# Layer 1's modulation vectors: from TensorE products in its branches to VectorE row sums in the two feed-forward loops

## The chip, the cores and the metric

One core of a Trainium2 chip runs the kernel. The metric is the device time of one execution in microseconds, as a median over runs. The engines are named as the profile names them: PE (TensorE matmul, with PEld for its weight loads), DVE (VectorE), ACT (ScalarE), POOL (GpSimd) and SP (SyncE, which here issues nearly all DMAs).

## The reference

Two layers of a diffusion backbone work on 384 tokens (256 latent, 128 context) of width 1024, in float32. Six modulation vectors of 1024 values, each in two versions (context `c_ctx` and latent `c`), steer a layer:

```python
mod_ctx = (jax.nn.silu(c_ctx) @ w_mod[l] + b_mod[l])[None, :]
mod_lat = jax.nn.silu(c) @ w_mod[l] + b_mod[l]
sh1, sc1, g1, sh2, sc2, g2 = [m[:, None, :] for m in jnp.split(mod, 6, axis=-1)]
h = layer_norm(x) * (1 + sc1) + sh1
x = layer_norm(ALPHA * x + g1 * (merged @ p["w_o"]), p["ln1_g"], p["ln1_b"])
h = layer_norm(x) * (1 + sc2) + sh2
x = layer_norm(ALPHA * x + g2 * ((jax.nn.silu(ug) * uv) @ p["w_down"]), p["ln2_g"], p["ln2_b"])
```

`merged` is the gated sum of three branches (attention, convolution module, Fourier mixing). `ug` and `uv` are the halves of a width-3 convolution of `h @ w_up` (2 x 2816 wide). The modulation depends on `c` and the weights alone, so it can be computed at any time before its use.

## The kernel before, in words

Every large product is made of three fp32r products of high and low halves (`mm3`, L196 to L198). The halves of a weight tile come from `halves`: ACT writes the high half (L179), DVE the low one (L180). Weight tiles come in through SP into 3 buffers `raw` of 1 MB; 5 buffers each hold high and low halves.

A layer has a mixing part (`mixing`) and a feed-forward part (the rest of `layer`). The mixing part makes the input projection, then three branches of eight steps each (`branch`); scores, values and the convolution (62 instructions of DVE a layer, L783 and L785) are written in between the steps. Then come the product with `w_o`, a closing normalization (`close`, L817 to L828) of three token tiles, and the feed-forward loop of 11 units. A unit makes four tiles of `w_up` (24 products each, `ws_tile`, into 2 PSUM buffers `ps`), empties each by ACT (L927) and DVE (L928, L930), gates them (L945 to L951) and multiplies with two row blocks of `w_down` (`down`). The products of the last five row blocks are held back (`TAIL`), to run between the end of the loop and `close`.

The modulation is computed in three ways. Kind A is shift and scale of the mixing part, B those of the feed-forward part, G the two gates.

- Layer 0, kind A: at the start, on PE (`mod_first`).
- Kinds G and B of both layers: in the branches of the same layer, on PE (`mod_stream`, L217). A step is 8 multiplications with a 32-column left side, which the profile shows as 16 matmuls; every second step of a branch calls one. Its weights come as 256 KB tiles into buffers `s2`. Gates go through a DRAM tile (`mod_gates`, L268 to L276, into `gscr`), from where `gate_bc` reads them back, spread over 128 partitions, before each `close`; shift and scale are copied (L282), transposed on PE (L286) and get their bias (L294).
- Layer 1, kind A: row sums on DVE in layer 0's feed-forward loop (`mod_rows`, L315). The weights lie transposed; one instruction multiplies a 128 x 1024 tile with `silu(c)`, spread over the partitions, and sums each row. There are 16 tiles with two sums each, so 32 sums. `next(rows, None)` takes one tile in each half unit from unit 2 on. The weights come as 512 KB tiles into two buffers, a fetch two tiles ahead.

`silu(c)` is made in `setup`: a load of `c2` (L145), DVE L146, ACT L147, DVE L148. It is written to DRAM (`cscr`, L154) for the row sums. That write stands in SP's queue between the loads of the tokens and those of all weights.

Each engine takes its instructions in a fixed order. The order is set before the run by a planner (the Tile framework), which goes by the order of writing but lets a later instruction pass where it takes an engine to be free and the later one to be ready. Buffers are handed out by tag (`s4` has 8, `ps` 2, `acc` 6); an instruction that needs a buffer waits until its last user is done.

Of the kernel before, what the change touches and what calls it, by code (L numbers as in the profile page):

```python
# [16 lines left out]
P = 128  # L17
# [60 lines left out]
class Net:  # L78
# [3 lines left out]
    def __init__(self, ctx, tc, a):  # L82
# [5 lines left out]
        self.modcol, self.bmod, self.colsets = {}, {}, {}  # L88

# [41 lines left out]
    def setup(self):  # L131
# [22 lines left out]
        nc.sync.dma_start(self.cscr.rearrange("v (k p) -> (v k) p", p=P), ch)  # L154
# [141 lines left out]
    def mod_rows(self, l, kind):  # L296

        nc, a = self.nc, self.a
# [3 lines left out]
        b0 = 3 if kind == "B" else 0  # L302
        tiles = [(j, k) for j in range(2) for k in range(KD)]
        sums = [self.sm(16) for _ in range(2)]

        def fetch(n):
            j, k = tiles[n]
            self.load(w[n % 2], a["w_modr"][l - 1, self.MODS[kind], j, k])
# [4 lines left out]
        for n, (j, k) in enumerate(tiles):  # L313
            for v in range(2):
                nc.vector.scalar_tensor_tensor(prod, w[n % 2], 1.0, cb[v], op0=ALU.mult, op1=ALU.mult,  # L315
                                               accum_out=sums[j][:, v * KD + k:v * KD + k + 1])
            if n + 2 < len(tiles):
                fetch(n + 2)
            if k == KD - 1:
                for v in range(2):  # L320
                    nc.vector.tensor_tensor(self.modcol[l][:, j + (2 if kind == "B" else 0), v, :],
                                            sums[j][:, v * KD:(v + 1) * KD], self.bmod[l][:, j + b0, :], op=ALU.add)
            yield

# [184 lines left out]
    def mixing(self, l, first, hT, mods):  # L509
# [63 lines left out]
        mods = self.mod_stream(mods)  # L573
# [3 lines left out]

        ci = conv_in()
# [23 lines left out]
        for i, _ in enumerate(branch(1, 0, "w_a", 4, aT, lambda: values(3))):  # L602
            next(cb, None)
            if i % 2:
                mod()
        for i, _ in enumerate(branch(2, 1, "w_c", 2, cT, lambda: [None for _ in cb])):
            if i % 2:
                mod()
        for _ in mods:
            pass  # L610
        return m_hl
# [233 lines left out]
    def layer(self, l, first, hT, mods):  # L845
        nc, a = self.nc, self.a
        m_hl = self.mixing(l, first, hT, mods)
# [59 lines left out]
        rows = self.mod_rows(l + 1, "A") if l + 1 < DEPTH else iter(())  # L907
# [188 lines left out]
```

## Time and profile before

| | |
|---|---|
| median of 3 runs | 1163.52 us (1162.24 to 1163.95) |
| the profiled execution | 1162.13 us, span 1160.3 us |
| PE busy | 1139.3 us (98%) |
| DVE busy | 785.1 us (68%) |
| ACT busy | 522.9 us (45%) |
| POOL busy | 77.5 us (7%) |

The span runs from the first to the last instruction; the time has some 1.8 us around it. Times in rows are microseconds from the span's start. PE is busy nearly all the time, so a microsecond of PE work that is taken out is one that can be won, if no other engine then stands in the way in the same stretch. In the stretch tables, a column is an engine's busy time with its number of instructions, then the clock granted to PE (1.00 is full), the mean busy share of the 16 DMA engines and their rate. In a timeline, a row is start, duration, engine, line, operation, and in brackets the idle time before it with what ended it.

### The profile page before, as it was taken

The page shows a single profiled execution, that of the slowest core. Times are in us where ns is not written, and L with a number is a line of the kernel's source. Part 1 is how long each engine was busy: PE and PEld are TensorE (multiplying, and loading weights), DVE is VectorE, ACT ScalarE, POOL GpSimd, SP SyncE. Part 2 cuts the span into 40 slices and gives each one's busy share as a digit, 9 for nine tenths or more (in the row PEclk, how much of TensorE's full clock was granted, in tenths as well). Part 3 has the DMA queues.
Part 4 walks back from the last instruction along what each step waited for, and adds up shares of the span by engine and source line. Part 5 has one row for each costly group of instructions (what it writes and reads, how often), then busy time and mean ns, then how long its engine had stood idle before and what let it go on. Part 6 is the DMA issues. An engine that isn't in the chain of part 4 may idle for free.

```text
span 1160.3 us, 16670 instructions
## 1 busy us (share of the span) xinstructions
PE 1139.3 (98%) x6569; PEld 1019.4 (88%) x6569; DVE 785.1 (68%) x1332; ACT 522.9 (45%) x875; POOL 77.5 (7%) x91
## 2 busy tenths in 40 slices
PE   8999999999999999999999999999999999999996
PEld 6788888898999999999958978889989999999995
DVE  5579965445799976666776799444477666555667
ACT  2457743242754344444372766233447444334440
POOL 1010001121100000000021000111110000000001
PEclk9999999999999999999999999999999999999998
DMA  9764567633366663343335364783427333333411
GB/s 362 295 205 145 167 229 271 231 141 127 128 236 206 229 206 139 109 136 119 110 122 216 118 218 155 277 313 109 146 73 251 112 114 141 113 142 109 146 37 55
DMA packets 47806, 195.95 MB, mean 169 GB/s; under 512 B 5552, under 2 KB 6608, under 8 KB 32624
## 3 DMA queue, kind: packets, MB, share of 16 engines
q1 hardware_dynamic: 47296, 194.10, 47.3%
q8 instruction: 52, 0.85, 0.3%
q10 hardware_dynamic: 432, 0.79, 0.2%
q14 instruction: 26, 0.21, 0.0%
HBM read 191.41 MB, written 3.45 MB: 168 GB/s over the span
## 4 chain that ended last, share of the span: by engine, by line
PE 84%; DVE 8%; ACT 2%; DMA 2%; POOL 1%; issue 1%; SPq 0%; POOLq 0%; DVEq 0%; ACTq 0%
PE ps L196 16%; PE ps L198 16%; PE ps L197 16%; PE acc L196 9%; PE acc L197 9%; PE acc L198 9%; PE acc L217 2%; PE acc L767 1%; DVE sm L372 1%; DVE wlo L180 1%; POOL sm L376 1%; DVE s L818 1%; DVE s L828 1%; PE acc L755 1%; ACT whi L179 1%
## 5 line engine op out<-in xcount | busy, mean ns | idle before, releaser
L180 DVE TENSOR_TENSOR wlo<-raw,whi 128x1024 fp32r<-128x1024 f32 x216 | 269.1, 1247 | 236.2 <-ACT whi L179 227.2
L196 PE MATMUL ps<-hT,whi 128*128 128x386 f32 (+1 forms) x1088 | 370.3, 340 | 1.8 <-ACT g L548 1.5
L198 PE MATMUL ps<-hT,wlo 128*128 128x386 f32 (+1 forms) x1088 | 368.7, 339 | 0.0
L197 PE MATMUL ps<-hT,whi 128*128 128x386 f32 (+1 forms) x1088 | 368.4, 339 | 0.0
L179 ACT CAST whi<-raw 128x1024 fp32r<-128x1024 f32 x216 | 225.8, 1049 | 308.1 <-PE ps L197 211.4
L196 PEld LDWEIGHTS ps<-hT,whi 128*128 128x128 f32 x1088 | 205.2, 189 | 14.1 <-ACT whi L179 5.0
L197 PEld LDWEIGHTS ps<-hT,whi 128*128 128x128 f32 x1088 | 205.2, 189 | 2.7 <-issue 1.7
L198 PEld LDWEIGHTS ps<-hT,wlo 128*128 128x128 f32 x1088 | 205.3, 189 | 0.3 <-issue 0.3
L197 PE MATMUL acc<-wlo,r 128*128 128x512 f32 x360 | 142.3, 395 | 0.0
L196 PE MATMUL acc<-whi,r 128*128 128x512 f32 x360 | 142.1, 395 | 0.0
L198 PE MATMUL acc<-whi,r 128*128 128x512 f32 x360 | 141.9, 394 | 0.0
L198 PEld LDWEIGHTS acc<-whi,r 128*128 128x128 f32 x360 | 67.6, 188 | 16.2 <-DVE r L951 0.5
L196 PEld LDWEIGHTS acc<-whi,r 128*128 128x128 f32 x360 | 67.6, 188 | 14.9
L197 PEld LDWEIGHTS acc<-wlo,r 128*128 128x128 f32 x360 | 67.6, 188 | 14.4
L785 DVE SCALAR_TENSOR_TENSOR cv<-upad,cst,cv 128x399 f32<-128x399 f32 x120 | 70.1, 627 | 0.1
L376 POOL TENSOR_TENSOR sm<-sm,mhalf 128x1 f32<-128x1 f32 x21 | 23.0, 1099 | 612.4 <-DVE sm L375 611.7
L950 ACT CAST r<-g 128x386 fp32r<-128x386 f32 x44 | 22.7, 515 | 89.5 <-DVE g L948 89.5
L927 ACT ACTIVATE g<-ps,cst 128x386 f32<-128x386 f32 x84 | 56.3, 670 | 0.0
L930 DVE SCALAR_TENSOR_TENSOR g<-ps,cst,g 128x385 f32<-128x385 f32 x84 | 52.0, 619 | 2.3
L928 DVE SCALAR_TENSOR_TENSOR g<-ps,cst,g 128x385 f32<-128x385 f32 x84 | 51.6, 614 | 0.2
L563 POOL TENSOR_TENSOR g<-g,g 128x384 f32<-128x384 f32 x32 | 35.8, 1118 | 181.8 <-DVE g L562 173.3
L945 ACT ACTIVATE g<-g 128x386 f32<-128x386 f32 x44 | 23.2, 527 | 45.2 <-DVE g L930 45.2
(185 smaller groups left out, 1353.0 us busy)
## 6 DMA issues: line engine op xcount, KB each, us to landing
raw<-w_u SPq DMA_DIRECT2D x44, 1024.0 KB, 4.8
s<-w_mod SPq DMA_DIRECT2D x128, 256.0 KB, 4.4
raw<-w_g SPq DMA_DIRECT2D x24, 1024.0 KB, 7.8
raw<-w_d SPq DMA_DIRECT2D x22, 1024.0 KB, 4.9
raw<-w_mod SPq DMA_DIRECT2D x8, 1024.0 KB, 9.5
raw<-w_o SPq DMA_DIRECT2D x8, 1024.0 KB, 4.8
s<-w_modr SPq DMA_DIRECT2D x16, 512.0 KB, 4.2
s<-w_z SPq DMA_DIRECT2D x8, 512.0 KB, 9.7
```

Of the source, the lines that this page charges most:

```text
L179: self.nc.scalar.copy(hi, raw)
L180: self.nc.vector.tensor_tensor(lo, raw, f32(hi), op=ALU.subtract)
L196: mm(ps, lh, rh, start=first, stop=False)
L197: mm(ps, lh, rl, start=False, stop=False)
L198: mm(ps, ll, rh, start=False, stop=last)
L217: self.nc.tensor.matmul(ps[32 * i:32 * i + 32, 0:n], self.cpad[:, k, :], src[k, i], start=ks[0] == 0 and k == ks[-1], stop=ks[-1] == KD - ...
L376: nc.gpsimd.tensor_tensor(mv[:, 3:4], mv[:, 2:3], self.mhalf, op=ALU.pow)
L563: nc.gpsimd.tensor_tensor(merged[m], merged[m], gt, op=ALU.add)
L785: nc.vector.scalar_tensor_tensor(c, u[:, i:i + CV_W], w, c, op0=ALU.mult, op1=ALU.add)
L927: nc.scalar.activation(c, ps, AF.Identity, bias=cols["ffn_b"][:, i:i + 1], scale=w[1])
L928: nc.vector.scalar_tensor_tensor(c[:, 1:NPAD], ps[:, 0:NPAD - 1], w[0], c[:, 1:NPAD], op0=ALU.mult, op1=ALU.add)
L930: nc.vector.scalar_tensor_tensor(c[:, 0:NPAD - 1], ps[:, 1:NPAD], w[2], c[:, 0:NPAD - 1], op0=ALU.mult, op1=ALU.add)
```

## The change

- `mods` for layer 1 is now empty: no `mod_stream` in its branches.
- `mod_rows` takes a list of units (layer, kind, which of the pair), each of 8 tiles and 16 sums. In layer 0's loop there are five: A 0, A 1, G 0, B 0, B 1, so 80 sums. In layer 1's loop there is one: G 1, so 16 sums. `mix_rows` (sums in the branches) is empty.
- `paced` spreads the steps over slots, one slot for each half unit from unit 1 on: 41 steps (the first only fetches) over 17 slots in layer 0, 9 steps over 9 slots in layer 1.
- `gate_rows` turns the sums of a gate into rows: a transpose on PE, a copy on ACT, an 8 KB write to `gscr`. It is called in the last unit of either feed-forward loop.
- The write of `cscr` moves from `setup` to `setup_late`, which comes after the loads of the input projection.

```diff
-        nc.sync.dma_start(self.cscr.rearrange("v (k p) -> (v k) p", p=P), ch)
+        self.silu = ch
...
     def setup_late(self):
         nc, a = self.nc, self.a
+        nc.sync.dma_start(self.cscr.rearrange("v (k p) -> (v k) p", p=P), self.silu)
...
+    def gate_rows(self, tag):
+
+        nc = self.nc
+        for l, j, cols in self.gate_sums:
+            pt = self.psum(tag)[0:2 * KD, 0:P]
+            nc.tensor.transpose(pt, cols, self.ident)
+            row = self.kk()[0:2 * KD, :]
+            nc.scalar.copy(row, pt)
+            nc.sync.dma_start(self.gscr[l, j].rearrange("v (k p) -> (v k) p", p=P), row)
+        self.gate_sums = []
+
+    def paced(self, units, slots):
+
+        steps = self.mod_rows(units) if units else iter(())
+        need, done = len(units) * KD + 1, [0, 0]
+
+        def step():
+            done[0] += 1
+            while done[1] * slots < need * done[0]:
+                done[1] += 1
+                next(steps, None)
+
+        return step
...
-        rows = self.mod_rows(l + 1, "A") if l + 1 < DEPTH else iter(())
+        step_rows = self.paced(rows, 17 if len(rows) > 1 else 9)
...
-                if u >= 2:
-                    next(rows, None)
+                if u >= 1:
+                    step_rows()
             if u >= 1:
                 down(u - 1)
+            if u == KF // 2 - 1:
+                self.gate_rows("ps")
         down(KF // 2 - 1)
         gate = self.gate_bc(l, 1)
...
-        mods = [[(0, "G"), (0, "B")], [(1, "G"), (1, "B")]]
+        mods = [[(0, "G"), (0, "B")], []]
+        mix_rows = [[], []]
+        ffn_rows = [[(1, "A", 0), (1, "A", 1), (1, "G", 0), (1, "B", 0), (1, "B", 1)], [(1, "G", 1)]]
```

## Rows read from the trace of the kernel before

**Rows 1.** The page's first part.

```profile
PE 1139.3 (98%) x6569; PEld 1019.4 (88%) x6569; DVE 785.1 (68%) x1332; ACT 522.9 (45%) x875; POOL 77.5 (7%) x91
```

**Rows 2.** Layer 1's branches by stretch: PE, PEld, DVE, ACT, POOL, clock, DMA share, GB/s.

```profile
664.00:720.00 56.00, 55.27 (x356) 46.35 (x355) 53.22 (x122) 37.87 (x95) 0.00 (x0) 1.00 0.56 188
720.00:792.00 72.00, 71.58 (x444) 61.58 (x443) 35.70 (x55) 25.76 (x39) 10.17 (x12) 1.00 0.71 256
```

**Rows 3.** The same stretches, L217 alone (PE busy, PEld busy).

```profile
664.00:720.00 56.00, 6.18 (x48) 1.05 (x48) 1.00 0.56 188
720.00:792.00 72.00, 9.62 (x80) 2.09 (x80) 1.00 0.71 256
```

**Rows 4.** Timeline of PE, the end of layer 1's modulation.

```profile
788.73 0.66 PE L286 MATMUL acc<-ident,s 128*128 128x128 f32 x4 [0.39 <-DVE s L282]
```

**Rows 5.** Busy times by stretch in layer 0's feed-forward loop, columns as in rows 2.

```profile
338.00:419.30 81.30, 81.30 (x425) 75.85 (x424) 77.98 (x126) 33.33 (x45) 0.00 (x0) 1.00 0.64 218
...
444.64:469.96 25.32, 25.32 (x133) 23.71 (x133) 15.23 (x20) 10.46 (x15) 0.00 (x0) 1.00 0.36 124
```

**Rows 6.** L315 alone in the first of these stretches (DVE busy, two records a sum).

```profile
338.00:419.30 81.30, 34.26 (x56) 1.00 0.64 218
```

**Rows 7.** Groups by line and shape, DVE, 325 to 570 us: the two records of a row sum.

```profile
L315 DVE SCALAR_TENSOR_TENSOR s<-s,s 128x1024 f32<-128x1024 f32 x29 | 35.2, 1216 | 0.1
...
L315 DVE DVE_READ_ACCUMULATOR s<-s,s 128x1 f32 x29 | 2.4, 81 | 0.0
```

**Rows 8.** Timeline of DVE: one row sum and its successor.

```profile
338.06 1.22 DVE L315 SCALAR_TENSOR_TENSOR s<-s,s 128x1024 f32<-128x1024 f32 x1
339.20 0.08 DVE L315 DVE_READ_ACCUMULATOR s<-s,s 128x1 f32 x1
339.20 0.56 DVE L948 TENSOR_TENSOR g<-g,g 128x386 f32<-128x386 f32 x1
```

**Rows 9.** Timelines, start of layer 0's feed-forward loop: first sum (DVE), first loop product (PE).

```profile
318.91 1.23 DVE L315 SCALAR_TENSOR_TENSOR s<-s,s 128x1024 f32<-128x1024 f32 x1 [0.65 <-DMA s<-w_modr]
...
324.97 0.42 PE L196 MATMUL ps<-hT,whi 128*128 128x386 f32 x1 [0.33 <-DVE g L930]
```

**Rows 10.** Timeline of SP's queue at the start.

```profile
2.12 0.43 SPq L121 DMA_DIRECT2D s<-x_p  x1
5.53 0.33 SPq L154 DMA_DIRECT2D cscr<-kk  x1
5.90 0.42 SPq L121 DMA_DIRECT2D s<-par  x1
```

**Rows 11.** Timeline of PE at the start, and busy times of this stretch (columns as in rows 2).

```profile
13.82 1.08 PE L217 MATMUL ps<-raw,cpad 128*32 128x128 f32 x32 [1.20 <-DMA raw<-w_mod]
...
19.06 0.51 PE L196 MATMUL acc<-whi,hT 128*128 128x512 f32 x1 [0.86 <-ACT hT L416]
...
10.86:19.06 8.20, 4.23 (x76) 2.81 (x77) 5.79 (x22) 3.37 (x6) 0.55 (x1) 1.00 1.01 422
```

**Rows 12.** Timelines at the end of layer 1's loop (PE, ACT, DVE).

```profile
1129.30 0.34 PE L198 MATMUL ps<-hT,wlo 128*128 128x386 f32 x1
...
1130.45 0.67 ACT L927 ACTIVATE g<-ps,cst 128x386 f32<-128x386 f32 x1
...
1135.32 0.69 DVE L817 TENSOR_TENSOR s<-acc,s 128x512 f32<-128x512 f32 x1 [0.58 <-PE acc L198]
...
1150.66 0.69 DVE L817 TENSOR_TENSOR s<-acc,s 128x512 f32<-128x512 f32 x1 [0.26 <-PE acc L198]
```

**Rows 13.** Busy times by stretch between these two L817, columns as in rows 2.

```profile
1135.30:1150.60 15.30, 15.30 (x66) 12.04 (x65) 14.76 (x24) 0.00 (x0) 3.04 (x2) 1.00 0.14 50
```

**Rows 14.** DMA issues: count, size of one, median us from issue to landing; one tile's extremes.

```profile
s<-gscr SPq DMA_DIRECT2D x8, 512.0 KB, 6.5
...
o_xs<-s SPq DMA_DIRECT2D x2, 256.0 KB, 2.1
...
DMA to landing us min/median/max: 4.1/6.5/7.3
```

More of the change, by code (lines that the diff above doesn't have):

```diff
@@ L301, in mod_rows, with fetch @@
         w = [self.s4() for _ in range(2)]
[L302 to L308, printed above, removed]
+        tiles = [(n, k) for n in range(len(units)) for k in range(KD)]
+        sums = [self.sm(16) for _ in units]
+        def fetch(i):
+            n, k = tiles[i]
+            l, kind, j = units[n]
+            self.load(w[i % 2], self.a["w_modr"][l, self.MODS[kind], j, k])
         fetch(0)
@@ L312, in mod_rows @@
         yield
-        for n, (j, k) in enumerate(tiles):
+        for i, (n, k) in enumerate(tiles):
             for v in range(2):
[L315 to L318, printed above, removed]
+                nc.vector.scalar_tensor_tensor(prod, w[i % 2], 1.0, cb[v], op0=ALU.mult, op1=ALU.mult,
+                                               accum_out=sums[n][:, v * KD + k:v * KD + k + 1])
+            if i + 2 < len(tiles):
+                fetch(i + 2)
             if k == KD - 1:
+                l, kind, j = units[n]
+                bias = self.bmod[l][:, {"A": (0, 1), "B": (3, 4), "G": (2, 5)}[kind][j], :]
+                dst = sums[n] if kind == "G" else self.modcol[l][:, j + (2 if kind == "B" else 0)]
                 for v in range(2):
-                    nc.vector.tensor_tensor(self.modcol[l][:, j + (2 if kind == "B" else 0), v, :],
-                                            sums[j][:, v * KD:(v + 1) * KD], self.bmod[l][:, j + b0, :], op=ALU.add)
+                    d = dst[:, v * KD:(v + 1) * KD] if kind == "G" else dst[:, v, :]
+                    nc.vector.tensor_tensor(d, sums[n][:, v * KD:(v + 1) * KD], bias, op=ALU.add)
+                if kind == "G":
+                    self.gate_sums.append((l, j, sums[n]))
             yield
+    def gate_rows(self, tag):
+        nc = self.nc
+        for l, j, cols in self.gate_sums:
[4 more added lines that the diff above has]
+            nc.sync.dma_start(self.gscr[l, j].rearrange("v (k p) -> (v k) p", p=P), row)
+        self.gate_sums = []
+    def paced(self, units, slots):
[7 more added lines that the diff above has]
+        return step
     def gate_bc(self, l, j):
@@ L506, in start_next, with mixing @@
         self.b_out(l, 1, acc, z, bb)
-    def mixing(self, l, first, hT, mods):
+    def mixing(self, l, first, hT, mods, rows):
         nc, a = self.nc, self.a
@@ L572, in mixing @@
             self.columns(l + 1)
-        mods = self.mod_stream(mods)
+        mods = self.mod_stream(mods) if mods else iter(())
         def mod():
             next(mods, None)
+        step_rows = self.paced(rows, 10)
         ci = conv_in()
@@ L610, in mixing @@
             pass
+        self.gate_rows("acc")
         return m_hl
@@ L843, with layer @@
     NF = 4
-    def layer(self, l, first, hT, mods):
+    def layer(self, l, first, hT, mods, mix_rows, rows):
         nc, a = self.nc, self.a
-        m_hl = self.mixing(l, first, hT, mods)
+        m_hl = self.mixing(l, first, hT, mods, mix_rows)
         gate = self.gate_bc(l, 0)
@@ L1012, in run @@
             self.norm(x, x, D)
-        mods = [[(0, "G"), (0, "B")], [(1, "G"), (1, "B")]]
+        mods = [[(0, "G"), (0, "B")], []]
+        mix_rows = [[], []]
+        ffn_rows = [[(1, "A", 0), (1, "A", 1), (1, "G", 0), (1, "B", 0), (1, "B", 1)], [(1, "G", 1)]]
         first, hT = xhat, self.new_hT(0)
         for l in range(DEPTH):
-            first, hT = self.layer(l, first, hT, mods[l])
+            first, hT = self.layer(l, first, hT, mods[l], mix_rows[l], ffn_rows[l])
 @with_exitstack
```

8 lines of the change are left out of this document (5 added, 3 removed).

## The prediction, made before the changed kernel ran

> **What bounds the kernel now.** I read the page's first part, then busy times by stretch, then timelines where an engine is full or waits. The page says that PE is the bound as a whole, busy 98% [rows 1], so the first question is where PE work goes away and whether another engine is full there. In layer 1's branches, 664 to 720 us, both are nearly full: PE is idle 56 - 55.27 = 0.7 us, but DVE only 56 - 53.22 = 2.8 us. From 720 to 792 us DVE has half its time free [rows 2]. In layer 0's feed-forward loop the 32 row sums of today do not spread over the loop: the first stands at 318.91, before the loop's first product [rows 9], and 28 of them run from 338 to 419.3 us. DVE is busy there 77.98 of 81.3 us, and still PE is busy all 81.30 [rows 5, 6]. Later, a unit of the loop lasts 25.32 us and asks 15.23 us of DVE [rows 5]. This is the row that matters most: DVE can be 96% busy without PE losing anything, yet 4% is all that is left.
>
> **The change part by part.** The sum is made against the profiled execution's own 1162.13 us, which is 1.39 below the median.
>
> *Layer 1's products taken out.* L217 occupies PE 6.18 us in the first stretch and 9.62 us in the second [rows 3]. The four transposes at the end cost a wait of 0.39 and 0.66 us of work, whose last part overlaps what follows [rows 4]; I count 0.8. Their 64 loads, the row addition (L273), the copy (L282) and the bias go too; they lie beside PE work. In the second stretch I count all: 9.6 + 0.8. In the first, DVE's work stays, so the stretch can shrink by no more than the 2.8 us that DVE is idle, unless convolution instructions move behind 720 us. I take 2.8. Together **-13.2**. The bounds: -10.4 if the first stretch gives nothing, -16.6 if it gives all 6.18.
>
> *Layer 0's loop.* Sums go from 32 to 80. There are 41 steps in 17 slots, of which 40 hold two sums, so 80 sums in 17 half units, or 9.4 a unit while they last. What does one cost? L315 lasts 1.216 us and its accumulator record 0.081 [rows 7], but the next instruction starts 1.14 us after the sum did, before it has ended [rows 8]. By busy time it is 34.26/28 = 1.22 us [rows 6]. The page "VectorE: DVE Perf Modes" of the Trainium skill, in "The DRAIN you can't avoid", says that the next operation does not start until the pipeline is empty; by that a sum would cost its two records, 1.30 us, and the place of this is the first rival below. The trace before shows 1.14 to 1.22.
>
> At what rate can DVE take them? It took 28 in 81.3 us beside all else, which is 8.7 in a unit of 25.32 us, with 3.3 us idle, or 1.0 a unit. If the idle time could all be used, it would be 8.7 + 1.0/1.22 = 9.6. So the need of 9.4 lies just below what DVE can give. Sums written early now fill gaps, as last choice; in the changed kernel they are written about as fast as gaps come, so some 0.7 a unit (9.4 - 8.7) go ahead of work that is written after them: the low halves of later weights, which have five buffers of slack, and L928 and L930, which empty `ps` and have only two. Over 8.5 units that is 6 sums, or 7.3 us of DVE work that must find its place in 8.5 us of idle time. Bounds: 0, if it does, since PE lost nothing at 96%, and +7.3, if PE waits for all of it. I take **+3**, nearer the stretch in which PE lost nothing, because after the last slot DVE has 10 us free a unit. The 24 additional loads of 512 KB go through SP between the weights' loads; they replace as many bytes in layer 1's branches, and the DMA engines were 64% busy in the stretch with sums [rows 5]. SP waits for a free buffer before each; behind it stand loads of `w_u` and `w_d`. At today's rate of sums this cost PE nothing, so nothing is counted. The buffers of `silu(c)` and the products now stay until the last sum, so the loads of the gate and the normalization rows come only behind it, still before the close. The transpose of gate G 0 costs 0.3.
>
> *Layer 1's loop.* 16 sums, 16 x 1.22 = 20 us of DVE, in a loop whose DVE load is as in the sum-free units: hidden in the 10 us a unit. The first of them stand before the loop as in layer 0, where PE waited 0.33 us for L930 right behind them [rows 9]: **+0.3**.
>
> *The last gate's way.* Its sums are done early, but `gate_rows` is written in the last unit, and PE keeps to the order there. So the transpose comes after the last `ps` product, which ends at 1129.64. Then come a copy on ACT behind L927, which starts at 1130.45 and lasts 0.67, so the copy ends at some 1131.4; a write of 8 KB; and only then two loads of 512 KB that wait for it. The trace shows no landing for a write this small. The nearest row is the 256 KB store of `o_xs`, 2.1 us [rows 14], and the bounds are 1 and 4. A gate load takes 4.1 at best, 7.3 at worst [rows 14]; nothing else loads there, so I take 4.1 and 0.5 for being the second. So the gate is there at 1131.4 + 2.1 + 4.6 = 1138.1, with waits of SP 1138.5 to 1139.5. L817 needs it at 1135.32 [rows 12]. That is 4.2 late at the end of the range. Can the close catch up? From the first L817 to that of the last tile, DVE is busy 14.76 of 15.3 us [rows 12, 13], so no: all but 0.3 reaches the end. Hence **+3.9**; bounds 0 (the planner pulls the transpose forward) and +7.
>
> *The start.* SP issues the tokens' last load at 2.12, then waits until 5.53 for `silu(c)` before any weight load; the next, `par`, goes out at 5.90 [rows 10]. Without the write there, everything behind it can go out some 3.3 us earlier. PE has 8.20 - 4.23 = 4.0 us idle between its warming products and 19.06, but only 1.2 of that waits for a DMA [rows 11]; the rest waits for DVE and ACT. I take **-1.2**; bounds 0 and -3.3. The write itself now goes out behind loads, long before its first reader.
>
> The sum: -13.2 + 3 + 0.3 + 0.3 + 3.9 - 1.2 = -6.9, so 1155.2 against 1162.13, and **1156.6** against the median.
>
> **The rivals.**
>
> *DVE becomes the bound of layer 0's loop (slower).* If each sum costs its full two records, a unit asks 15.23 + 9.4 x 1.297 = 27.4 us of DVE, which is 2.1 more than PE's 25.32. Over 8.5 units that is +17.9 in place of +3: 1162.13 - 6.9 + 14.9, and 1.4 to the median, gives **1171.5**. For it: the need lies at the edge of what was shown, and a planner that runs DVE full has no room for its own errors. Against it: the successor that starts before the sum has ended [rows 8], and 81 us without any loss of PE [rows 5]. It decides the sign from +10 in this loop on (the other terms sum to -9.9). By the Trainium skill's page named above it would be so; the trace, by rows 8, does not agree.
>
> *Layer 1's branches give little (no change).* The steps of L217 may stand where PE would else wait for a copy or a low half, so that taking one out opens a wait. If only half of the second stretch's 9.6 is won and nothing at its end, the gain is 2.8 + 4.8 = 7.6 in place of 13.2, and the sum is -1.3: **1162.2**. For it: DVE has next to nothing free before 720 [rows 2], and its arrears would be due behind. Against it: DVE at half load there.
>
> *All of it is hidden (faster still).* The planner spreads the sums into gaps, pulls the gate's transpose forward, and moves convolution behind: -15.5 + 0.3 + 0.3 - 1.2 = -16.1, **1147.4**. For it: sums did move forward, from unit 2 to before the loop [rows 9]. Against it: PE's queue showed no such moves late in a loop.
>
> **How the numbers follow.** A measurement of this kernel can tell some 0.2% from no change, 2.3 us: below 1161.2 is faster, above 1165.8 slower. The forecast has 0.60, nearly all of it faster (below 1161.2 for all but the worst of its bounds); the hidden case 0.11, faster; the branches' case 0.12, about half of it within 0.2%; DVE as the bound 0.17, slower. So 0.69 faster, 0.11 the same, 0.20 slower. The range goes from 1147, the hidden case, to 1170, most of the way into the slower one. The likeliest case's own range is 1149 to 1163: the branches at their two bounds, -16.6 and -10.4, with some of the others.
>
> **What would show it.** In the changed profile: L217 only in layer 0, and the stretch from layer 1's first score to `w_o` shorter by 10 to 16 us; in layer 0's loop 80 sums, a start-to-start of 1.14 to 1.3 us, PE busy near 100%, and a loop not over 7.3 us longer; L817 of layer 1's last close waiting 3 to 6 us for a DMA of `gscr`; the first w_mod product not waiting. I would be wrong if PE shows waits for DVE L928 or L930 or for low halves through layer 0's loop, or if the branches shorten by less than 10 us.

## The result, and the profile after

The changed kernel takes **1149.21 us** (median of 4 runs, 1148.54 to 1149.61) against 1163.74 for the kernel before on the same chip: a ratio of 0.9876, 95% interval [0.986, 0.9891]. That is 14.5 us less, where the forecast was 6.9. The profiled execution took 1149.61, with a span of 1147.7, so it lies 12.5 below that of before.

Lines have moved by a few: L196 to L198 are now L198 to L200, L217 is L219, L315 is L318, L785 is L822, L817 is L854, L900 is L937, L928 and L930 are L965 and L967. The page's first part, to be read beside [rows 1]:

```profile
PE 1124.1 (98%) x6439; PEld 1015.9 (89%) x6439; DVE 847.5 (74%) x1462; ACT 522.1 (45%) x877; POOL 79.0 (7%) x90
```

PE lost 130 matmuls and 15.2 us of busy time, DVE gained 62.4 us. To see where the time went, I cut the span at PE instructions that both kernels have, and compare the lengths (us). The `ps<-s,raw` products (L937) are the first `w_up` tiles of a loop, in three groups, one for each token tile; the third group's start is the cut. `acc<-raw,s` is the next layer's input projection.

| stage, from and to | before | after | difference | forecast |
|---|---|---|---|---|
| start, to layer 0's first score product (`acc<-kT,r`) | 88.59 | 89.12 | +0.5 | -1.2 |
| layer 0's loop, third group `ps<-s,raw` to first `acc<-raw,s` | 270.65 | 272.45 | +1.8 | +3.3 |
| layer 1's scores, first to eighth score | 62.20 | 57.52 | -4.7 | -2.8 |
| rest of layer 1's branches, to L937 (L900) | 149.59 | 138.43 | -11.2 | -10.4 |
| layer 1's loop, to PE's last instruction | 269.14 | 269.32 | +0.2 | +0.3 |
| PE's last instruction to the end of the span | 9.6 | 10.4 | +0.8 | +3.9 |

All other stages agree within 0.1 us. The branches are the gain. Busy times of their two stages (columns as in [rows 2], cut at the same instructions), first before:

```profile
652.71:714.91 62.20, 61.47 (x392) 52.55 (x391) 59.23 (x138) 43.37 (x105) 0.00 (x0) 1.00 0.50 165
714.91:864.50 149.59, 149.17 (x843) 132.73 (x843) 79.36 (x128) 55.69 (x88) 23.59 (x23) 1.00 0.52 186
```

and after:

```profile
655.07:712.59 57.52, 56.78 (x344) 51.62 (x343) 54.78 (x131) 43.32 (x105) 0.00 (x0) 1.00 0.16 56
712.59:851.02 138.43, 138.43 (x760) 130.44 (x760) 82.12 (x130) 55.68 (x88) 24.98 (x22) 1.00 0.41 141
```

Beside the scores PE has 48 matmuls fewer and the stage is shorter by just PE's busy time (61.47 - 56.78 = 4.69). DVE is still idle for 57.52 - 54.78 = 2.7 us, where the forecast had it use up all of its idle time. It stays idle because 4.5 us of its work is no longer there, most of it convolution. This alone (L785, now L822), before and after, is

```profile
652.71:714.91 62.20, 29.69 (x51) 1.00 0.50 165
```

```profile
655.07:712.59 57.52, 26.16 (x45) 1.00 0.16 56
712.59:851.02 138.43, 8.80 (x14) 1.00 0.41 141
```

so six convolution instructions (3.5 us) moved behind the scores, into a stage with DVE idle for 56 us.

Layer 0's loop, in the stretch of [rows 5], all instructions and then the sums alone ([rows 6]):

```profile
338.00:419.30 81.30, 81.30 (x426) 76.03 (x426) 79.58 (x130) 33.45 (x45) 0.00 (x0) 1.00 0.65 220
```

```profile
338.00:419.30 81.30, 34.56 (x59) 1.00 0.65 220
```

DVE is 98% busy and PE loses nothing here; the sums now go on until 540.5 us. PE's waits between 320 and 573 us, by what it waited for (total, times, longest), are few:

```profile
PE acc L199 <- DVE wlo L182: 0.9, 1, 0.9
PE ps L198 <- DVE g L967: 0.4, 2, 0.2
PE ps L198 <- ACT whi L181: 0.2, 1, 0.2
```

The end, against [rows 12]: the transpose (L338) stands at 1116.05, the gate's loads go out at 1119.27, and the first gate product waits for them. Timeline of SP's queue and of DVE:

```profile
1117.86 0.32 SPq L341 DMA_DIRECT2D gscr<-kk  x1
1119.27 0.81 SPq L122 DMA_DIRECT2D s<-gscr  x2
1124.57 1.29 DVE L854 TENSOR_TENSOR s<-acc,s 128x512 f32<-128x512 f32 x2 [3.26 <-DMA s<-gscr]
1125.78 1.28 DVE L855 SCALAR_TENSOR_TENSOR s<-s,s 128x512 f32<-128x512 f32 x2
1126.98 1.28 DVE L404 BATCH_NORM_STATS2 sm<-s 128x6 f32<-128x512 f32 x2
...
1135.85 1.28 DVE L857 SCALAR_TENSOR_TENSOR s<-s,sm,s 128x1024 f32<-128x1024 f32 x1
1137.35 0.69 DVE L854 TENSOR_TENSOR s<-acc,s 128x512 f32<-128x512 f32 x1 [0.21 <-PE acc L200]
1137.96 1.41 DVE L861 SCALAR_TENSOR_TENSOR s<-s,sm,s 128x512 f32<-128x512 f32 x2
...
1143.23 1.42 DVE L861 SCALAR_TENSOR_TENSOR s<-s,sm,s 128x512 f32<-128x512 f32 x2 [0.44 <-POOL sm L408]
```

Counted from the third group's start (881.48 before, 867.99 after), the first gate product (L854) comes at 256.58 in place of 253.84, so it is 2.7 late; the last one, the second half of the last tile's, comes at 269.36 in place of 269.18. Between them lie 12.78 us where it was 15.34, and DVE's busy time there shrank too, which shows against [rows 13]:

```profile
1124.57:1137.35 12.78, 12.74 (x55) 9.96 (x53) 12.56 (x23) 0.00 (x0) 2.79 (x2) 1.00 0.24 94
```

Two instructions (L861, 1.41 us) went behind the last gate product, and the other 22 (the 23 in the row take in the last gate product at its edge) follow each other faster, because the planner put them in another order. The kernel before does one half of a tile behind the other, so that most instructions need the result of the one just before:

```profile
1136.05 0.69 DVE L818 SCALAR_TENSOR_TENSOR s<-s,s 128x512 f32<-128x512 f32 x1
1136.71 0.69 DVE L817 TENSOR_TENSOR s<-acc,s 128x512 f32<-128x512 f32 x1
1137.32 0.69 DVE L372 BATCH_NORM_STATS2 sm<-s 128x6 f32<-128x512 f32 x1
1137.92 0.68 DVE L818 SCALAR_TENSOR_TENSOR s<-s,s 128x512 f32<-128x512 f32 x1
1138.63 0.69 DVE L372 BATCH_NORM_STATS2 sm<-s 128x6 f32<-128x512 f32 x1
...
1155.34 1.41 DVE L824 SCALAR_TENSOR_TENSOR s<-s,sm,s 128x512 f32<-128x512 f32 x2 [0.44 <-POOL sm L376]
```

In the changed kernel the two halves alternate (the pairs "x2"). A 512-wide instruction that doesn't need the result just before it starts 0.60 us after its predecessor (a pair takes 1.28), one that does 0.70 to 0.73 (L818 here at 1136.05, behind the L817 of [rows 12] at 1135.32). Both leave the same 0.69 in busy time. Of the 2.56 us between the two gate products the order is worth some 1.2 and the two L861, counted from start to start, 1.3; but these two must still be done, so the last pair comes 5.88 us behind the last gate product in place of 4.68.

At the start, SP's queue against [rows 10] goes straight through (`par` at 2.59 in place of 5.90):

```profile
2.59 0.43 SPq L122 DMA_DIRECT2D s<-par  x1
3.07 0.98 SPq L122 DMA_DIRECT2D raw<-w_mod  x2
```

and still PE's first `w_mod` products wait, 0.87 us for DVE and 0.98 for a DMA, where [rows 11] had 1.20 for a DMA:

```profile
11.13 1.08 PE L219 MATMUL ps<-raw,cpad 128*32 128x128 f32 x32 [0.87 <-DVE cpad L152]
13.19 1.08 PE L219 MATMUL ps<-raw,cpad 128*32 128x128 f32 x32 [0.98 <-DMA raw<-w_mod]
```

PE's first `w_z` product comes at 18.66 in place of 19.06, so 0.4 was won up to there. The loss lies behind it: over the next six us PE is busy throughout in both kernels, but the clock granted to it was 0.72 of full before and 0.50 after, which is the level of 1.2 GHz. PE's last two waits before that were 1.06 and 1.10 us, and 1.16 and 0.86 in the kernel before (columns as in [rows 2], first before, then after):

```profile
19.06:25.06 6.00, 6.00 (x45) 3.88 (x46) 2.32 (x5) 2.05 (x4) 0.00 (x0) 0.72 1.02 418
```

```profile
18.66:24.66 6.00, 6.00 (x41) 4.26 (x42) 2.31 (x5) 2.05 (x4) 0.00 (x0) 0.50 1.02 416
```

### The profile page after: what moved, and what is told of

Read it like the earlier page. It is cut to its first block, busy times and chain, and to the rows that moved or that the text cites. A ratio compares the mean times of both kernels' runs of the same rounds, so it can differ in the third digit from the quotient of the medians.

```text
span 1147.7 us, 16506 instructions
## 1 busy us (share of the span) xinstructions
PE 1124.1 (98%) x6439; PEld 1015.9 (89%) x6439; DVE 847.5 (74%) x1462; ACT 522.1 (45%) x877; POOL 79.0 (7%) x90
## 4 chain that ended last, share of the span: by engine, by line
PE 81%; DVE 9%; DMA 3%; ACT 3%; issue 2%; POOL 1%; SPq 0%; POOLq 0%; DVEq 0%; ACTq 0%
PE ps L198 16%; PE ps L200 16%; PE ps L199 16%; PE acc L198 9%; PE acc L199 9%; PE acc L200 9%; PE acc L804 1%; DVE s L318 1%; PE acc L219 1%; DMA s<-w_z 1%; DVE wlo L182 1%; DVE sm L404 1%; ACT whi L181 1%; DVE s L855 1%; POOL sm L408 1%
## 5 line engine op out<-in xcount | busy, mean ns | idle before, releaser
L198 PE MATMUL ps<-hT,whi 128*128 128x386 f32 (+1 forms) x1088 | 370.3, 340 | 2.0 <-ACT g L580 1.5
L200 PE MATMUL ps<-hT,wlo 128*128 128x386 f32 (+1 forms) x1088 | 368.4, 339 | 0.0
L198 PEld LDWEIGHTS ps<-hT,whi 128*128 128x128 f32 x1088 | 205.1, 189 | 11.4 <-issue 3.9
L200 PEld LDWEIGHTS ps<-hT,wlo 128*128 128x128 f32 x1088 | 205.2, 189 | 0.8 <-issue 0.7
L200 PE MATMUL acc<-whi,r 128*128 128x512 f32 x360 | 141.4, 394 | 0.0
L198 PE MATMUL acc<-whi,r 128*128 128x512 f32 x360 | 140.5, 396 | 0.0
L318 DVE SCALAR_TENSOR_TENSOR s<-s,s 128x1024 f32<-128x1024 f32 x96 | 116.8, 1217 | 0.6 <-DMA s<-w_modr 0.5
L200 PEld LDWEIGHTS acc<-whi,r 128*128 128x128 f32 x360 | 67.6, 188 | 15.5
L198 PEld LDWEIGHTS acc<-whi,r 128*128 128x128 f32 x360 | 67.6, 188 | 15.1 <-ACT r L987 0.5
L822 DVE SCALAR_TENSOR_TENSOR cv<-upad,cst,cv 128x399 f32<-128x399 f32 x120 | 70.7, 634 | 0.1
L965 DVE SCALAR_TENSOR_TENSOR g<-ps,cst,g 128x385 f32<-128x385 f32 x84 | 51.6, 614 | 2.8 <-ACT g L964 2.7
L967 DVE SCALAR_TENSOR_TENSOR g<-ps,cst,g 128x385 f32<-128x385 f32 x84 | 51.9, 617 | 1.3
```

The source lines that it names most:

```text
L198: mm(ps, lh, rh, start=first, stop=False)
L200: mm(ps, ll, rh, start=False, stop=last)
L318: nc.vector.scalar_tensor_tensor(prod, w[i % 2], 1.0, cb[v], op0=ALU.mult, op1=ALU.mult, accum_out=sums[n][:, v * KD + k:v * KD + k + 1])
L822: nc.vector.scalar_tensor_tensor(c, u[:, i:i + CV_W], w, c, op0=ALU.mult, op1=ALU.add)
L965: nc.vector.scalar_tensor_tensor(c[:, 1:NPAD], ps[:, 0:NPAD - 1], w[0], c[:, 1:NPAD], op0=ALU.mult, op1=ALU.add)
L967: nc.vector.scalar_tensor_tensor(c[:, 0:NPAD - 1], ps[:, 1:NPAD], w[2], c[:, 0:NPAD - 1], op0=ALU.mult, op1=ALU.add)
```

## The experiments

All stages are measured as above, in each run's own profile, with the branches in one (layer 1's first score to L937), so that a term is compared with its own stage and not with a whole run. "Sums" are those in layer 0's loop, in layer 1's branches and in layer 1's loop; the slots are those of layer 0. Each ratio is to runs of the kernel before beside it, whose medians go from 1162.16 to 1163.74, so medians of two rows may differ by 1.6 for that alone.

| run | sums | start | loop 0 | branches | end | median | ratio to before |
|---|---|---|---|---|---|---|---|
| before | 32 / 0 / 0 | 88.59 | 270.65 | 211.79 | 9.6 | 1163.74 | 1 |
| after | 80 / 0 / 16 | 89.12 | 272.45 | 195.95 | 10.4 | 1149.21 | 0.9876 |
| e1, early write | same | 89.83 | 273.13 | 195.94 | 10.4 | 1150.64 | 0.9896 |
| e2, early transpose | same | 87.54 | 271.97 | 195.94 | 9.4 | 1146.89 | 0.9869 |
| e3, products kept | 80 / 0 / 0 | 88.64 | 274.55 | 211.87 | 9.5 | 1165.96 | 1.0031 |
| e4, gates kept | 64 / 0 / 0 | 87.90 | 270.39 | 202.62 | 9.2 | 1151.29 | 0.9902 |
| e5, all in loop 0 | 96 / 0 / 0 | 87.38 | 293.17 | 195.96 | 9.4 | 1167.85 | 1.0053 |
| e7, gate in branches | 80 / 16 / 0 | 88.05 | 272.22 | 196.25 | 9.2 | 1146.95 | 0.9867 |
| e8, only the write | 32 / 0 / 0 | 88.06 | 270.09 | 211.80 | 9.3 | 1161.01 | 0.9985 |
| e9, late transpose | 80 / 0 / 16 | 87.87 | 273.11 | 195.96 | 10.4 | 1148.09 | 0.9875 |
| e10, two more hops | same | 86.99 | 272.82 | 195.95 | 12.9 | 1149.82 | 0.9890 |
| e11, spread | 64 / 16 / 16 | 87.86 | 270.33 | 196.12 | 9.1 | 1145.13 | 0.9850 |
| e12, gate in scores | 80 / 16 / 0 | 87.75 | 273.17 | 226.02 | 9.2 | 1176.70 | 1.0129 |
| e13, e7 and 20 slots | 80 / 16 / 0 | 87.34 | 270.46 | 196.25 | 9.2 | 1144.89 | 0.9851 |
| e14, e15, untied | 80 / 0 / 16 | 90.89, 91.13 | 273.22, 273.56 | 195.94, 195.96 | 10.4, 10.4 | 1151.89, 1152.61 | 0.9905, 0.9912 |
| e16, tied, 16 | same | 87.98 | 273.47 | 195.18 | 10.8 | 1148.73 | 0.9881 |
| e17, tied, 48 | same | 87.57 | 272.56 | 202.88 | 10.4 | 1156.08 | 0.9943 |

**The start.** The write of `silu(c)` back in its old place (e1), and the kernel before with this write alone moved (e8).

```diff
-        self.silu = ch
+        nc.sync.dma_start(self.cscr.rearrange("v (k p) -> (v k) p", p=P), ch)
```

> The changed kernel with one part undone: the write of silu(c) stands at the start again, ahead of the weights' loads. Reading of the result (theory A): the earlier loads won 0.4 us up to PE's first w_z product (18.66 instead of 19.06 us) and lost it again, with 0.5 more, to the clock, which was granted at 0.50 from 18 to 24 us instead of 22 to 24. So undoing it gives about -0.6 us: 1148.6, and the first L937 of layer 0 at 300.3 instead of 300.8. Theory B (the prediction): earlier loads win 1.2, so undoing them gives +1.2: 1150.4, and L937 at 302.0.

> The kernel before with only the write of silu(c) moved behind the first loads. Against the kernel before. Theory A (this is the start's share of the change): first scores 0.5 to 1.3 us earlier than 88.59 give or take the 1 us by which the start varies, all else equal; in all -0.5 to -1.3, ratio 0.9989 to 0.9996. Theory B (the start waits for VectorE and ScalarE, not for the loads): 0. Theory C (the move has a cost later, the first w_mod products or the sums wait for the write's new place): +1 or more.

e1's ratio to the kernel before is 0.9896 [0.9879, 0.9912] where the changed kernel has 0.9876 [0.986, 0.9891], so its loss is not clear by itself. e8 is faster than before, ratio 0.9985 [0.9977, 0.9994], so 0.7 to 2.7 us. The start itself varies by 2 us between profiles: with the write moved, and nothing added there, 14 profiles give 86.99 to 89.12, mean 87.86; with it early, two give 88.59 and 89.83. The profiled execution of the changed kernel is the slowest of the 14, and the only one with a granted clock of 0.50 over the six us behind its first `w_z` product: the other 13 have 0.64 to 0.77. Why it was lower there is open. So theory A of e1 read that one profile rightly, but what it saw is not what the move does. The moved write is worth about 1.3 us on the mean; theories B and C of e8 fall, and theory A of e1.

**The last gate.** Its transpose in an earlier unit (e2), later (e9), and with two more transfers in its way (e10).

```diff
-            if u == KF // 2 - 1:
+            if u == (6 if l else KF // 2 - 1):
```

> The changed kernel with the last gate's transpose, copy and write in unit 6 of layer 1's feed-forward loop instead of the last unit. The close then finds its gate loaded, and its first L854 waits for PE and no longer 3.3 us for gscr. Theory A: the late gate cost 2.8 us at the first close, of which the close won back 2.1, so -0.7: 1148.5. Theory B (the prediction): the close cannot win anything back, so -2.6 to -2.8: 1146.5. Rival C: the transpose in the middle of the loop takes a ps buffer and costs PE as much as it saves: no change.

```diff
-            if u == KF // 2 - 1:
+            if u == KF // 2 - 1 and not l:
                 self.gate_rows("ps")
         down(KF // 2 - 1)
+        self.gate_rows("ps")
```

> In layer 1 the last gate's transpose is issued after the last down products instead of before them, so the gate arrives later by the PE work in between, 3 to 5 us. Against the changed kernel, by the time from the last product to the end of the span and from the third down product on. Theory A (the close can win back only the 2.1 to 2.6 us by which its dependent instructions follow one another faster when they are late, and the changed kernel has used that up): the first gate product moves by 3 to 5 us and the end by as much, first to last gate product stays at 12.5 to 12.8 us. Theory B (lateness is absorbed in part at every step): the end moves by half of it, 1.5 to 2.5 us. Theory C (nothing waits for it): 0.

```diff
+            if (l, j) == (1, 1):
+                hop = self.dr.tile([2, D], F32, tag="hop", name="hop", bufs=1)
+                nc.sync.dma_start(hop.rearrange("v (k p) -> (v k) p", p=P), row)
+                row = self.kk()[0:2 * KD, :]
+                nc.sync.dma_start(row, hop.rearrange("v (k p) -> (v k) p", p=P))
             nc.sync.dma_start(self.gscr[l, j].rearrange("v (k p) -> (v k) p", p=P), row)
```

> The last gate's rows go through two more small transfers (written, read back, written again) before the two gate loads, so that the gate is later by the landings of two transfers of 8 KB, an estimated 3 to 5 us from the 1.4 us median landing of the write and SP's issue and wait around each. Against the changed kernel. Theory A (the close has one reserve, the 2 to 2.6 us that its short dependent instructions gain when they follow one another, and the changed kernel uses it up): the first gate product moves by 3 to 5 us, first to last gate product stays between 12.3 and 12.8 us, the time from the last PE instruction and the whole run grow by 3 to 5. Theory B (part of any lateness is absorbed): the run grows by half of it, 1.5 to 2.5. Theory C (the gate was not what the close waited for): 0.

In e2 the first gate product waits for PE as before, the order on DVE is again that of the kernel before, and the end is 1.0 shorter: the term was +1.0, near theory A, so B and C fall.

```profile
1119.90 0.69 DVE L854 TENSOR_TENSOR s<-acc,s 128x512 f32<-128x512 f32 x1 [0.59 <-PE acc L200]
```

e9's edit changed nothing: the planner leaves the transpose where it was in PE's order, and the end is the same 10.4. So e9 tests none of its theories. In e10 the first gate product is 3.0 later than in the changed kernel (259.54 from the third group's start):

```profile
1120.46 0.81 SPq L122 DMA_DIRECT2D s<-gscr  x2
...
1125.73 1.29 DVE L859 TENSOR_TENSOR s<-acc,s 128x512 f32<-128x512 f32 x2 [6.25 <-DMA s<-gscr]
```

and the end is 2.4 longer. So of the first 2.7 us of lateness the close wins back 1.7 to 2.0, of the next 3.0 only 0.6. Neither theory holds as written: 2.4 lies below A's 3 to 5 and within B's range, and from the first to the last gate product it is 10.55 us, not A's 12.3 to 12.8, because still more instructions went behind the last gate product. What A had right is that the reserve is nearly used up.

**The products and the sums apart.** Both (e3), and the gate's products alone kept on PE (e4).

```diff
-        mods = [[(0, "G"), (0, "B")], []]
+        mods = [[(0, "G"), (0, "B")], [(1, "G"), (1, "B")]]
...
-        ffn_rows = [[(1, "A", 0), (1, "A", 1), (1, "G", 0), (1, "B", 0), (1, "B", 1)], [(1, "G", 1)]]
+        ffn_rows = [[(1, "A", 0), (1, "A", 1), (1, "G", 0), (1, "B", 0), (1, "B", 1)], []]
```

> The 80 row sums in layer 0's loop as in the changed kernel, and layer 1's products in its branches as before (both write the same values; the 16 sums in layer 1's loop are left out). This measures the sums alone. Theory A: +0.6 at the start and +1.8 in layer 0's loop, and layer 1's branches as long as before to 0.5 us: 1166.1 against 1163.7 (+2.4). Theory B (the prediction's price): +3.3 in the loop: about 1167. Theory C (every sum at its two full records): +17.9: 1181.

```diff
-        mods = [[(0, "G"), (0, "B")], []]
+        mods = [[(0, "G"), (0, "B")], [(1, "G")]]
...
-        ffn_rows = [[(1, "A", 0), (1, "A", 1), (1, "G", 0), (1, "B", 0), (1, "B", 1)], [(1, "G", 1)]]
+        ffn_rows = [[(1, "A", 0), (1, "A", 1), (1, "B", 0), (1, "B", 1)], []]
```

> Both gates of layer 1 on PE in its branches again (the first four of the eight steps of products, which lie in the stretch up to the last scores, where DVE is full), shift and scale of the feed-forward part as sums (64 sums in layer 0's loop, none in layer 1's). Theory A (a product taken out wins its PE time in full, because convolution instructions move behind the scores): the branches become 7.7 us longer than in the changed kernel, the loop about 1.2 shorter, the end 0.7 shorter: 1155.0. Theory B (the prediction: this stretch wins only what DVE had idle, 2.8 us): the branches become 2.8 to 4.5 us longer: 1150.1 to 1151.8.

With the products back the branches are as long as before (211.87), whatever DVE does elsewhere: the whole gain lies in PE's products. In e3 the sums, with nothing in return, make the time 1.0031 [1.0017, 1.0045] times that of the kernel before, so theory C falls. Its loop costs 3.9, over both A's 1.8 and B's 3.3, and is the longest of all with these sums; PE waits 2.3 us for L967 in it, in place of 0.4 in the changed kernel, and why is open. In e4 the loop with 64 sums costs nothing against 32 (270.39 against 270.65), and the gates' products 6.7 us of branches, nearer to A's 7.7 than to B's 2.8 to 4.5: the scores alone are back at 62.26, with 51 convolution instructions in them. At this pace the cost of 80 sums is that of the last 16.

**How many sums, and how fast.** All 96 in layer 0's loop (e5); 80 over more slots, with the last gate in the branches (e13, and e7 for the second part alone); 64, 16 and 16 (e11, with e2's edit).

```diff
-(1, "B", 0), (1, "B", 1)], [(1, "G", 1)]]
+(1, "B", 0), (1, "B", 1), (1, "G", 1)], []]
```

> The last gate's 16 sums go into layer 0's feed-forward loop too (96 sums there, none in layer 1's). Against the changed kernel. Theory A (DVE is the limit of that loop only as long as it has nothing free; it is full to about 520 us and has some 9 us free from 520 to 573, so 16 more sums, 16 x 1.22 = 19.5 us, fill these and the rest is waited for): the loop 3 to 9 us longer than the 272.5 of the changed kernel, the end 0.7 to 1.0 us shorter, layer 1's loop 0.2 shorter; in all +2 to +8. Theory B (the planner still puts all sums into gaps, since 64 to 80 sums cost only 2 us): loop +0.6 or less, in all -0.5 to -1. Theory C (every sum beyond capacity is paid in full): loop +19.5, in all +18.

```diff
-        mix_rows = [[], []]
+        mix_rows = [[], [(1, "G", 1)]]
...
-(1, "B", 1)], [(1, "G", 1)]]
+(1, "B", 1)], []]
```

> The last gate's 16 sums go into layer 1's branches, over their 10 late steps, and none into layer 1's loop; its transpose, copy and write then stand at the end of the branches. Against the changed kernel. Theory A (DVE has half its time free behind the first part of the branches): 19.5 us of sums hide there, the rest of the branches (138.43 in the changed kernel) no more than 0.6 longer for one transpose, the end 1.0 shorter as in the run with the early transpose, in all -0.4 to -1. Theory B (convolution that moved behind the scores now fills that half, so the sums push it on): the rest +3 to +8, in all +2 to +7.

e13 has this too, and:

```diff
-        step_rows = self.paced(rows, 17 if len(rows) > 1 else 9)
+        step_rows = self.paced(rows, 20 if len(rows) > 1 else 9)
```

> The last gate's sums in layer 1's branches as in the run before, and layer 0's 80 sums over 20 half units of its loop in place of 17, so 8.0 a unit in place of 9.4. Against that run (loop 272.22, 1146.95). Theory A (VectorE takes some 9.6 sums a unit with everything in gaps; at 8.0 there is room, while 9.4 leaves none and 11.3 cost 20.7 us): loop 270.2 to 270.8, in all -1.4 to -2. Theory B (the two microseconds of the loop are its start, where sums pile up before the first product, not the rate): loop 271.8 to 272.8, in all 0.

```diff
+        mix_rows = [[], [(1, "B", 1)]]
+        ffn_rows = [[(1, "A", 0), (1, "A", 1), (1, "G", 0), (1, "B", 0)], [(1, "G", 1)]]
...
+            if u == (6 if l else KF // 2 - 1):
```

> 64 sums in layer 0's feed-forward loop, 16 (B 1) in layer 1's branches, 16 (the last gate) in layer 1's loop with its transpose a few units early. Against the changed kernel. Theory A (by the runs so far: 64 sums cost layer 0's loop nothing, 16 in the branches 0.3, the early transpose gives 1.0): loop 270.1 to 270.7 in place of 272.5, the rest of the branches 138.4 to 138.8, the end 1.0 shorter, in all -2.5 to -3.2: 1146 to 1146.7 and the fastest version. Theory B (layer 0's loop varies by itself by 2 us, and its mean is not a matter of sums): loop 271.5 to 273, in all -1.

e5 falls off an edge: loop 0 is 20.7 us longer than with 80 sums, and theory C was nearest. The slots stayed 17, so 96 sums are 11.3 a unit over 8.5 units, more than the 9.6 that the forecast worked out as DVE's most; by this estimate (11.3 - 9.6) x 8.5 x 1.22 = 17.6 us are too much. PE's waits in this loop, 16 us in all; the rest of the loss is PE being busy for longer, 276.67 us in place of 270.92, in part at a lower clock (last section):

```profile
PE acc L199 <- DVE wlo L182: 12.5, 4, 5.0
PE ps L198 <- DVE g L967: 3.5, 3, 1.7
```

That the rate decides, and not the number, is shown by e13: the same 80 sums at 8.0 a unit in place of 9.4 cost nothing (270.46). The whole loop in the changed kernel, in e13 and in e5, one fence for each (columns as in [rows 2]):

```profile
317.78:590.23 272.45, 270.92 (x1430) 251.69 (x1431) 253.23 (x408) 116.00 (x169) 2.54 (x3) 1.00 0.61 208
```

```profile
316.00:586.46 270.46, 270.24 (x1430) 251.99 (x1431) 253.68 (x408) 115.96 (x169) 2.59 (x3) 1.00 0.61 209
```

```profile
316.02:609.19 293.17, 276.67 (x1430) 254.09 (x1431) 271.91 (x442) 116.74 (x170) 2.60 (x3) 0.98 0.61 207
```

DVE's busy time is the same in the first two, 253 us of 270; only its place differs. These rates are as written. In the traces, which are a little off them, the 80 sums run from 319.3 to 540.5 us in the changed kernel, 9.2 a unit, and from 317.6 to 554.7 in e13, 8.5 a unit. Over all runs, 80 sums in 17 slots give 271.97 to 273.56 (11 profiles without the products, mean 272.9); 32 sums, 64 in 17 slots and 80 in 20 give 270.09 to 270.65 (5 profiles, mean 270.4): +2.5 us. So theory B of e13 falls. e7 shows that 16 sums fit the late branches for 0.3 us, as its theory A had it, and e11's stages are those of its theory A. e13, 1144.89 (0.9851 [0.9836, 0.9866]), and e11, 1145.13 (0.985 [0.9835, 0.9864]), are the fastest versions. Their intervals just overlap that of the changed kernel, but the stages agree with a gain: in e13 -2.0 in loop 0, -1.2 at the end, +0.3 in the branches.

**Is DVE's idle time the bound beside the scores?** First with real sums (e12: as e7, but with `step_rows` called beside the eight scores), then with small instructions in place on a constant that is read no more, untied (e14, e15) and reading each score's `i3` (e16, e17).

```diff
-        step_rows = self.paced(rows, 10)
+        step_rows = self.paced(rows, 8)
...
                 values(i // 2)
             next(cb, None)
+            step_rows()
```

> The last gate's 16 sums stand in the first part of layer 1's branches, beside the scores, where VectorE has 2.7 us idle in 57.5, and not in layer 1's loop. Against the run with these sums in the late steps of the branches (scores 57.51, rest 138.74). Theory A (in this stretch VectorE's other work, convolution above all, moves behind it when it must, so its idle time is no bound): scores 57.5 to 58.5, the rest up to 140, fewer convolution instructions beside the scores than 45; in all 0 to +1. Theory B (VectorE's idle time bounds the stretch, as the forecast had it: 19.5 us of sums into 2.7 us): scores +10 to +17.

```diff
+            for _ in range(6 if l else 0):
+                nc.vector.scalar_tensor_tensor(self.zeros, self.zeros, i3[:, 0:1], self.zeros, op0=ALU.mult, op1=ALU.add)
             prob[h] = [d for d, _ in pss]
```

This is e17; e16 has 2 in place of 6, and e14 and e15 have 2 and 6 with 1.0 for the scalar, beside the call of `scores` in place of within it.

> The changed kernel with 16 small VectorE instructions (128x128, in place on a constant tile that is read no more, two beside each score) in the first part of layer 1's branches; they use no buffer that anything waits for. Each an estimated 0.2 to 0.3 us (between the 0.16 us of a 128x8 addition and the 0.29 us of a 128x128 reduction in this stretch), so 3.2 to 4.8 us, against 2.74 us of VectorE idle in 57.52. Theory A (idle time is no bound there: convolution moves behind the scores when VectorE is full): scores 57.5 to 57.8, fewer than 45 convolution instructions in them, all else equal, 0. Theory B (idle time is the bound, as the forecast had it): scores +0.5 to +2.1.

> The same with 48, six beside each score: 9.6 to 14.4 us of VectorE work against 2.74 us idle. Theory A: scores 57.5 to 58, convolution instructions in them down from 45 to about 25 to 32, the rest of the branches still 138.4 to 139, in all 0 to +1. Theory B: scores +7 to +12.

> As the run with 16 small VectorE instructions, but each reads the reciprocal sums of its score, so that it can't be issued before that score. 14 of them (0.29 us each, 4.1 us) stand before the last score, and in VectorE's written order six convolution instructions fewer do (40 for 46). Theory A (convolution gives way, idle time is no bound): the scores 57.5 to 57.8, convolution in them 39 for 45, the rest of the branches 138.4. Theory B (idle time of 2.74 us is the bound): scores +1.3 to +1.9.

> The same with 48, of which 42 (12.2 us) stand before the last score, and 37 convolution instructions in place of 46 (9 fewer, 5.2 us at 0.58). Theory A (convolution gives way as far as the written order moves it, and the rest must find VectorE idle): 12.2 - 5.2 - 2.7 = 4.3, so scores +2 to +5, the rest 138.4 to 139.4. Theory B (idle time is the bound, what moves does not count): +9.4, in all +9. Theory C (still hidden in full): 0 to +0.5.

e12 lost 30 us in the branches, more than both theories, by a third way: one wait. Timelines of PE and ACT:

```profile
709.87 1.11 PE L802 MATMUL acc<-s,s 128*64 128x256 f32 x2 [28.07 <-ACT s L793]
```

```profile
709.23 0.58 ACT L793 COPY s<-acc 128x512 f32<-128x512 f32 x1 [26.53 <-DVE s L318]
```

ACT's copy of the attention's probabilities needs an `s4` buffer, and of the eight the sums keep five until the last of them is done. So e12 says nothing of DVE's idle time. Nor do e14 and e15: with nothing to tie them to the scores, the planner issued the added instructions at the start, from 12.2 us on in e14, where PE's first `w_z` product came 3.1 us later than in the changed kernel (21.79 against 18.66). e16 tells it apart. Busy times of its scores and of the rest, and convolution (L824 there) alone:

```profile
654.95:711.47 56.52, 55.78 (x344) 52.09 (x344) 54.17 (x138) 43.65 (x105) 0.00 (x0) 1.00 0.17 57
711.47:850.13 138.66, 138.66 (x759) 130.45 (x759) 87.25 (x138) 55.70 (x88) 23.76 (x22) 1.00 0.40 141
```

```profile
654.95:711.47 56.52, 22.94 (x39) 1.00 0.17 57
```

Work for 4.8 us was added to DVE, more than its 2.7 us idle; convolution went from 45 to 39 instructions, DVE is still idle for 2.4 us, and the stage didn't grow. Theory B falls. With three times as much (e17) the branches are 6.9 us longer. Up to the eighth score it is 3.9, as theory A had it (35 convolution instructions are left there), but the rest, which A had at 138.4 to 139.4, grew by 3.0 too:

```profile
653.61:715.06 61.45, 58.38 (x343) 51.24 (x343) 57.80 (x158) 42.20 (x102) 0.00 (x0) 1.00 0.14 44
715.06:856.49 141.43, 140.51 (x759) 130.39 (x759) 91.50 (x152) 57.05 (x91) 26.42 (x22) 1.00 0.40 142
```

So what convolution makes room for has an end, and past it the added work is paid in part; what the 3.0 behind the scores are, is not shown.

## Why the prediction was wrong in size

The direction and the sign of every term were right, and the time lies inside the range. The gain was twice the forecast, for two terms that were set too pessimistically, both on DVE. With the terms as the runs give them: -15.8 in the branches, +2.5 in loop 0, +0.2 in loop 1, +1.0 at the end, -1.3 at the start, in all -13.4; the profiles say -12.5, the medians -14.5.

- **Layer 1's products.** "The stretch can shrink by no more than the 2.8 us that DVE is idle, unless convolution instructions move behind 720 us. I take 2.8." The exception was what happened: -4.7, with six convolution instructions moved, and e16 shows the mechanism by itself. Where DVE's work in a stage is in part filler (due only later, and put wherever there is room), its idle time is not the bound, as far as the filler can move (e17 shows the end of that). The rest gave 11.2 for the 10.4 counted, so all of the forecast's upper bound of 16.6 but 0.8 was won. This is 2.6 us of the error.
- **The last gate's way.** The chain was right: the gate was 2.7 late, and the forecast's arrival at 1138.1 to 1139.5 was 2.8 to 4.2 late. That the low figure is met so closely is in part luck: the write took 1.4 us for 2.1, and from the loads' issue to the product it took 5.3 for 4.6. Two choices failed. It took the late end. And "DVE is busy 14.76 of 15.3 us, so no: all but 0.3 reaches the end" read busy time as work that can't be compressed. In a chain of short dependent instructions the start-to-start distance holds waiting that the busy column doesn't show, and the planner, which sets the order before the run, took it out; two instructions also went behind the last gate product. The cost was 0.8 (against the kernel before) to 1.0 (against e2) in place of 3.9: 2.9 to 3.1 us of the error.
- **Layer 0's loop.** Right: +3.3 forecast with the gate's transpose, +2.5 on the mean and +1.8 in this profile. The account by rate, a need of 9.4 sums a unit close under a capacity of 9.6, was sound: at 8.0 the loop costs nothing (e13), at 11.3 it costs 20.7 more (e5). The 9.6 itself no run fixes. A sum cost 1.14 to 1.22 us here, not 1.30: the 59 records of the stretch at 338 us are 34.56 us, or 29 sums and a half at 1.17. The rival "DVE becomes the bound" was real, and 16 sums away, but by the rate and not by a price of 1.30.
- **Layer 1's loop** cost 0.2 for 0.3. **The start** was right on the mean (-1.3 for -1.2), though one profile can't show it. The sign that the prediction named for it did not come: PE's first `w_mod` product still waited, 0.87 us, for DVE.
- The rival in which the branches give little fell with e3 and e4; the case "all of it is hidden" had the size of the branches right and, with 1147.4, lay nearer to the time than the forecast did.

The Trainium skill, "VectorE: DVE Perf Modes", "The DRAIN you can't avoid", says that the next operation does not start until the pipeline is empty, and adds that one that is not held starts earlier. The close agrees with the addition as far as it goes: 0.60 us from start to start where an instruction waits for nothing, before the 0.69 of its predecessor are over, and 0.70 to 0.73 where it needs the result just before it. What else may hold an instruction, no run here tests.

## What to carry to other kernels

Before an engine's idle time in a stretch is taken as the bound of a gain, see which of its instructions there are due in that stretch; filler moves, and the bound moves with it. Work for a nearly full engine is priced by its rate against the free rate, not by its sum: 80 row sums cost 2.5 us at 9.4 a unit, nothing at 8.0, and 96 at 11.3 some 20 us more. And look at the buffers that moved work holds: the same 16 sums cost 0.3 us in one half of the branches and 30 us in the other.

## What the runs showed of the hardware

In two runs PE paid twice for a long wait. In e5 a wait of 5.0 us left the next products at a lower clock: granted 0.60 on the mean from 404.55 to 408.50 (mostly 0.50, the level of 1.2 GHz), and 1.00 after that. At first they stand 0.43 us apart, later 0.23 (PE's timeline, and the two stretches):

```profile
404.55 0.79 PE L199 MATMUL acc<-wlo,r 128*128 128x512 f32 x1 [4.98 <-DVE wlo L182]
405.14 0.63 PE L200 MATMUL acc<-whi,r 128*128 128x512 f32 x1
405.57 0.63 PE L199 MATMUL acc<-wlo,r 128*128 128x512 f32 x1
```

```profile
404.55:408.50 3.95, 3.95 (x11) 3.14 (x12) 3.95 (x4) 0.00 (x0) 0.00 (x0) 0.60 0.77 304
408.50:412.00 3.50, 3.50 (x21) 3.41 (x20) 2.92 (x5) 0.03 (x1) 0.00 (x0) 1.00 1.02 360
```

Behind the 28 us of e12 the granted clock was 0.50, the level of 1.2 GHz, for 5.1 us (stretch of 709.87 to 715 us):

```profile
709.87:715.00 5.13, 5.13 (x15) 4.11 (x16) 5.01 (x15) 1.32 (x3) 0.00 (x0) 0.50 0.00 0
```

The 8 KB write of the gate took 1.4 us from issue to landing, below the 2.1 of the 256 KB store [rows 14] that stood in for it. DMA issues of the changed kernel: count, size of one, median us to landing:

```profile
gscr<-kk SPq DMA_DIRECT2D x2, 8.0 KB, 1.4
```
